# Value and gate blocks 512 columns wide over three token tiles, distance-16 scores copied by ScalarE, and seven raw places in the down-projection

## The chip, the cores and the metric

One core of one Trainium2 chip runs the whole step as one launch. The metric is the device time of that launch in microseconds (us). Time before the change: 1357.84 us, the median of 3 runs (1354.48 to 1359.75).

The engines are named as in the profile: PE is TensorE (matrix products, results in PSUM), PEld its weight loads, DVE is VectorE, ACT is ScalarE, POOL is GpSimd, SP is SyncE, which issues every DMA of this kernel from one in-order queue.

## The reference

One inference step of a one-layer hybrid encoder, on 1024 prompt frames (no history) and 32 sample frames (with states), float32 throughout. `D_MODEL` is 1024, `D_FF` is 2816.

```python
def mixer(xn, ...):                       # xn = rms_norm(x, g)
    proj = xn @ w_in                      # 1024 -> q, k, v, gates of three head groups
    # GLA (6 heads) and HGRN2 (5 heads): gated linear scans in blocks of 64 positions
    scores = jnp.einsum('bihd,bjhd,bijhd->bijh', qc, kc, decay)
    o = (jnp.einsum('bijh,bjhv->bihv', scores, vc)
         + jnp.einsum('bihk,bhkv->bihv', qc * jnp.exp(b), s))
    ...                                   # mLSTM (5 heads): stabilised scan of the same shape
    o = head_rms_norm(o, g) * silu(gate)  # the mLSTM's gate is a sigmoid
    return cat @ w_out, states

def conv_ffn(xn, buf, w_up, conv_w, conv_b, w_down):
    up = xn @ w_up                        # 1024 -> 2 x 2816
    up, buf = causal_dwconv(up, buf, conv_w, conv_b)   # width 3
    gate, val = jnp.split(up, 2, axis=-1)
    return (gelu(gate) * val) @ w_down, buf

x = x + rms_norm(mixer(rms_norm(x)), g_post)
x = x + rms_norm(conv_ffn(rms_norm(x)), g_post)
```

It returns the new frames, the states of the three head groups, and the last rows of both convolutions.

## The kernel before

**Products in three.** Every large product is done with operands split into a high half (a cast to float32r) and a low half (the rest): `mm3` (L88 to L91) issues high x high, high x low and low x high into the same accumulator. `split` (L95 and L98) makes the halves: a cast on ScalarE, a subtraction on VectorE. So each raw weight tile costs one ScalarE and one VectorE instruction before TensorE can use it. In groups 1 and 2 of the input projection the low halves come back from DRAM, where group 0 stored them (`lf_d`, `lt0_d`, `lt_d`; `kept`).

**Input projection, `inproj`.** Tokens are taken in three groups: 0 to 383, 384 to 767, and 768 to 1023 with the 32 sample frames. In each group the normalised frames lie in SBUF as `xh` and `xl`, features on partitions. First comes block 0 of the values for each token tile, then 13 feature blocks (`feat`), then the blocks 1 to 7 of 256 columns: blocks 0 to 3 hold values (`v_d`), 4 to 7 gates (`g_d`). In groups 0 and 1 `vg` goes through the token tiles one by one: 8 slices of the inner dimension, 3 matmuls each, one accumulator (`psb`, tag `big`, three banks in all), with the tile's frames as the stationary operand and 256 weight columns as the moving one. `vg_weights` loads a block as two pieces of [128, 4, 256] floats (`wr` raw, three places; `wh` and `wl`, four places each), and every token tile uses both pieces. `vg_store` reads the accumulator (a ScalarE copy for values; `tanh` into the single buffer `vth` and then a VectorE instruction for gates) and stores 128 x 256 floats. In group 2 `vg_across` does the same blocks with weights as the stationary operand.

**Mixer.** `mixer` handles one tile of 128 tokens, two chunks of 64. The scores within a chunk are built from six distances (32, 16, 8, 4, 2, 1), two to a PSUM tile `sc` of two banks, of which there is one. Per distance, VectorE and ScalarE make decayed copies of q and k, TensorE multiplies them in small tiles, and `copy_scores` puts the result into the matrix `P`: for distance 32 with two ScalarE copies of a rectangle, for the others with a predicated copy under a mask on VectorE (`put`, L808). The mixer of a group runs beside the input projection of the next, that of group 2 beside the output projection.

**Up-projection.** `up_all` runs 22 feature blocks, each as seven products of half size (Strassen's scheme) in 274 and 256 columns, then `up_finish` does the convolution, gelu and product into `h_d`, and sums of quarters of the activations (`s_d`, from tile `st`) and of the down-weights (`t_d`, from tiles `bw`).

**Down-projection, `down_all`.** The first part handles tokens of tiles 0, 8 and 4: 22 blocks, each loading 288 columns of activations (tag `hr`, two places) and a weight row (`wide`, four places, where weight sums are made too). Then `seven` handles the other six token tiles as seven products `p1` to `p7`. Each product has 11 tiles. A raw tile of 896 columns (`r`, tag `y0`, three places) gets 384 columns of activations and 512 of weights in two loads; both are split (`h_halves`, four places in two tags; `weight_halves`, seven places), and three accumulators of 512 columns get three matmuls each. The products run in the order p1, p2, p6, p5, p3, p7, p4; some accumulate onto a bank that an earlier product left, after ScalarE or VectorE has read it.

**Order of instructions.** `merge` and `pump` interleave emission of the mixer with the projections. After that a planner sets the order on every engine: `Graph` takes the dependencies (buffer reuse among them), `play` runs a list schedule with costs from `_cost`, `PRODUCT` (ns of a matmul by columns) and `PACKET` (DMA), the longest remaining path first, and `order` pins the result. In `play`, a load lands at the end of its turn in the DMA queue plus 650 ns.

Of the kernel before, what the change touches and what calls it, by code (L numbers as in the profile page):

```python
# [9 lines left out]
F32 = mybir.dt.float32  # L10
F32R = mybir.dt.float32r
# [20 lines left out]
NCOL = 2 * HW  # L32
# [9 lines left out]
def fcol(u):  # L42
# [24 lines left out]
VG0 = [range(0, 3), range(3, 6), range(6, 8)]  # L67

TC = dict(schedule_with_timeline_sim=True)
IN_NAMES = ["xp", "xs", "w_feat", "w_tok0", "w_tok", "w_out", "w_up", "w_dn", "vecs", "gcols", "grows", "wg",  # L70
            "mconv", "mcache", "fconv", "fcache", "s_gh", "s_c", "s_m", "rowb", "masks", "cf"]
OUTS = [
    ("yp", (SEQ, D)), ("ys", (DEC, D)),
# [6 lines left out]
def body(ctx: ExitStack, tc: tile.TileContext, a: dict):  # L80
    nc = tc.nc
    act, dve, pool, pe, sp = nc.scalar, nc.vector, nc.gpsimd, nc.tensor, nc.sync
# [21 lines left out]
    dr = ctx.enter_context(tc.tile_pool(name="dr", bufs=1, space=DRAM))  # L104
    cp = ctx.enter_context(tc.tile_pool(name="cp", bufs=1))
    psb = ctx.enter_context(tc.tile_pool(name="psb", bufs=3, space=PSUM))
# [6 lines left out]
    pa = pas.enter_context(tc.tile_pool(name="pa", bufs=1, side="right"))  # L113
# [17 lines left out]

    lf_d = dr.tile([13, 128, 8, 128], F32R, name="lf_d")
    lt0_d = dr.tile([128, 8, 282], F32R, name="lt0_d")
    lt_d = dr.tile([7, 2, 128, 4, 256], F32R, name="lt_d")

    def xsrc(t0, n):
        return a["xp"][t0:t0 + n, :] if t0 < SEQ else a["xs"][t0 - SEQ:t0 - SEQ + n, :]
# [25 lines left out]
    vecs = const("vecs_sb", [128, 12], F32, a["vecs"])  # L163
# [180 lines left out]
    def inproj(g, xh, xl, normed, scaled=None):  # L344
# [44 lines left out]

        def vg_weights(blk):  # L390
            parts = [(a["w_tok0"][:, ks[0]:ks[-1] + 1], ks, lt0_d[:, ks[0]:ks[-1] + 1]) for ks in VG0] if not blk else \
                [(a["w_tok"][blk - 1, hf], range(4 * hf, 4 * hf + 4), lt_d[blk - 1, hf]) for hf in range(2)]
            ws = []
            for i, (src, ks, low) in enumerate(parts):
                wh, wl, _ = weights(src, pa, f"wt{g}_{blk}_{i}", [128, len(ks), 256 if blk else 282],
                                    raw=wraw.pop((blk, i), None), eng=dve, low=low, kept=g > 0)
                ws += [(wh[:, k], wl[:, k]) for k in range(len(ks))]
            return ws
# [18 lines left out]
        def vg(blk):  # L417
            ws = vg_weights(blk)
            N = 256 if blk else 282
            for i, (u, off, n) in enumerate(units_of(g)):  # L420
                ps = psb.tile([128, N], F32, tag="big", name=f"pv{u}_{blk}")
                for k in range(8):
                    mm3(ps[:n, :N], (xh[:, k, off:off + n], xl[:, k, off:off + n]), ws[k], k == 0, k == 7)
                if not blk:
                    act.copy(tgs[:n, i, :], ps[:n, 256:])
                vg_store(blk, u, off, n, ps)
                yield

        def vg_across(blks):

# [225 lines left out]
        if sl:  # L656
            yield from vg_across(range(1, 8))
            return
        for blk in range(1, 8):
            yield from vg(blk)  # L660
            if blk == 5 and g < 2:
                for _ in scale_x(g + 1):
                    pass

# [6 lines left out]
    def mixer(u, g, ci0):  # L671
# [176 lines left out]
        def copy_scores(c, sc, lv):  # L848
            s = sc[:, :, 32 * lv:32 * lv + cl // 2]
            if c == levels[0]:  # L850
                for (o, m) in chunks:
                    act.copy(P[o:o + c, :, c:2 * c], s[o:o + c])
            else:
                put(c, s[:n])

# [449 lines left out]
    def down_all(ph, p6, gp):  # L1305
# [40 lines left out]
            return hh, hl  # L1346


        off, w = {}, 0
        for u in FIRST:  # L1350
            off[u] = w
# [2 lines left out]
        banks = [p.tile([128, 512], F32, tag=t, name=f"pd0_{i}", bufs=b) for i, (p, t, b) in enumerate(where)]  # L1354
        pair = []
        for f in range(NF):
            r = ph.tile([128, 288], F32, tag="hr", name=f"hr{f}", bufs=2)
            for u in FIRST:
                n = 128 if u < 8 else DEC
                sp.dma_start(r[:, off[u]:off[u] + n], h_d[f, :, fcol(u):fcol(u) + n])  # L1360
            hh, hl = h_halves(f"0_{f}", w, r, ph, "h")
            wr = praw[0].tile([128, 1024], F32, tag="raw", name=f"wd0_{f}r", bufs=2) if f < 2 else                 wide(f"wd0_{f}r")
            sp.dma_start(wr, a["w_dn"][f])
            wd = [weight_halves(f"wd0_{f}{hf}", wr[:, 512 * hf:512 * hf + 512]) for hf in range(2)]
            pair.append(wr)
            if f % 2:
                if f // 2 >= len(EARLY):
                    sums(f // 2, pair)
                pair = []
            if f == NF - 6:  # L1370
                sp.dma_start(gp, a["grows"][1:2, :].broadcast_to([128, 1024]))
                for u in FIRST:
                    residual(u)
            for d in range(8):
                c = slice(128 * (d % 4), 128 * (d % 4) + 128)
                mm3(banks[d][:, :w], [t[:, c] for t in wd[d // 4]], (hh[:, :w], hl[:, :w]), f == 0, f == NF - 1)
# [27 lines left out]
        def seven(p, ps, first):  # L1404
            ops = []
            for k in range(NP):
                r = ph.tile([128, NCOL], F32, tag="y0", name=f"r{p}_{k}", bufs=3)
                sp.dma_start(r[:, :384], ASRC[p](k))
                sp.dma_start(r[:, 384:896], BSRC[p](k))
                hh, hl = h_halves(f"{p}_{k}", 384, r[:, :384], *((ph, "h") if k % 2 else (p6, "g")))  # L1410
                wd = weight_halves(f"wd{p}_{k}", r[:, 384:896])
                ops.append((k, hh, hl, wd))
                if k == NP - 2:
                    continue
                for i in range(3):
                    c = slice(128 * i, 128 * i + 128)
                    for (j, hh, hl, wd) in ops:
                        mm3(ps[i], (hh[:, c], hl[:, c]), wd, first and j == 0, j == NP - 1, skip_group_check=True)
                ops = []
                if k % 3 == 0 and todo:  # L1420
                    todo.pop(0)()
# [54 lines left out]
    def merge(main, nmain, nside):  # L1476

        done = 0
        for i, _ in enumerate(main):
            want = (i + 1) * nside // nmain  # L1480
            pump(want - done)
            done = want
# [3 lines left out]
        return chain_of(*[mixer(u, g, c) for (u, c) in us[-1:] + us[:-1]]) if us[-1][0] == 8 else \  # L1486
            chain_of(*[mixer(u, g, c) for (u, c) in us])

    NMIX, NIN = 14, 12 + 2 + 24

    for g in range(3):
        xs_ = norm_tiles(g)
        n_side = (0, 3 * NMIX - 6, 3 * NMIX)[g]
        pump(1000)
        scaled = scale_x(0) if g == 0 else None
        if scaled:
            next(scaled)
            next(scaled)
        merge(inproj(g, *xs_, norm_group(g, *xs_), scaled), NIN, n_side)
        if g == 0:  # L1500
            mixer_zeros()
        side.append(mixers(g))
# [92 lines left out]
AHEAD = {"mx": 10000., "psm": 10000., "pdx0": 1400., "pdx1": 700., "pdw0": 1400., "pdw1": 700., "pt": 130000.}  # L1595
ENGINES = ("PE", "DVE", "Activation", "Pool", "SP")
WINDOW = 3413.3
PRODUCT = {512: 232., 384: 175.5, 288: 133.5, 282: 131.5, 274: 126.5, 256: 118.}
PACKET = ((4, 9), (32, 9), (128, 13), (256, 18), (512, 27), (1024, 46), (1536, 65), (2048, 84), (4096, 159), (8192, 330), (1 << 16, 2640))
TABLES = {"Ln": 5, "Gelu_apprx_tanh": 11, "Exp": 0, "Tanh": 0, "Square": 0}  # L1600

# [267 lines left out]
def play(g, tail, change, slack=None):  # L1869
# [32 lines left out]
    while True:  # L1902
# [30 lines left out]
        if e == "SP":  # L1933
            free[e] = t + own
            queue = max(t + 1400, queue) + d
            stop = queue + 650
        elif e == "PE":
            d, wide, m, cl, (row, sums) = mm[n]
            if mode not in (None, m):
                t = max(t, max(cells) + (93 if mode == (128, 128) else 45))  # L1940
            mode, t = m, max([t] + [cells[c] for c in cl])
            if wide:
                free[e] = clock.run(t, d)
                cells = [free[e]] * 16
                stop = free[e] + 166
            else:
                f = clock.factor(t)
                for c in cl:
                    cells[c] = t + d * f
                clock.add(t, 14)  # L1950
                free[e] = t + 14 * f
                stop = t + d * f + 168
        else:
            if e == "DVE" and lock:
                t = max(t, port["Pool"])
                port["DVE"] = t + d
            if e == "Pool" and lock == 1:
                port["Pool"] = t + d
            if g.table[n] not in (None, table):
                table = g.table[n]  # L1960
                t += 1283
            free[e], stop = t + own, t + d
# [26 lines left out]
def _layout(i):  # L1989
# [12 lines left out]
    wt = np.hstack([wv, np.hstack([gr, hg, mo])[:, of_plane]]).reshape(2, 4, 128, 8, 256)  # L2002
    wt = wt.transpose(3, 0, 2, 1, 4)
    w_tok = np.ascontiguousarray(wt[1:])
    w_tok0 = np.hstack([wv[:, :256], gg, mf, mi]).reshape(8, 128, 282).transpose(1, 0, 2)
    w_out = np.asarray(i["w_out"])[0][of_plane].reshape(8, 128, 1024)
    w_up = np.ascontiguousarray(np.asarray(i["ffn_w_up"])[0].reshape(8, 128, 44, 128).transpose(2, 1, 0, 3))
# [58 lines left out]
    for pl, (t, r0, dk) in enumerate(PLANES):  # L2066
        cf[r0:r0 + dk, 832 + 11 * t + pl] = 1.0
        if t < 2:
            cf[r0:r0 + dk, 876 + 2 * t + (r0 // 32 % 2 if dk == 32 else 0)] = 1.0
    r = dict(xp=np.asarray(i["x_prompt"])[0], xs=np.asarray(i["x_sample"])[0], w_feat=w_feat, w_tok0=w_tok0, w_tok=w_tok, w_out=w_out,  # L2070
             w_up=w_up, w_dn=w_dn, vecs=vecs, gcols=gcols, grows=grows, wg=wg, mconv=mconv, mcache=mcache, fconv=fconv,
             fcache=fcache, s_gh=s_gh, s_c=s_c, s_m=s_m, rowb=rowb, masks=masks, cf=cf)
    return {k: np.ascontiguousarray(v) for k, v in r.items()}
# [44 lines left out]
```

## Time and profile before

| | us |
|---|---|
| median of 3 runs | 1357.84 |
| the profiled execution | 1356.24 |
| its span, first to last instruction | 1354.4 |
| TensorE busy (modelled ends) | 1303.9 |
| VectorE busy | 1039.2 |
| ScalarE busy | 710.6 |

The stages in the profiled span: group 0 of the input projection up to some 160 us, group 1 to 340, group 2 to 475, output projection to 645, up-projection to some 1090, first part of the down-projection to 1171, the seven products to 1347, and the last sums and stores.

How to read the lines: in a table by stage, each engine has its busy us and, in brackets, its instructions; then the granted TensorE clock (1.00 is full), the mean busy share of the 16 DMA engines, and GB/s. A line of a tile has count, then shortest, median and longest duration in ns, the first and the last start in us, and the shapes. A line of waits reads: who waited, for whom, us in total, times, longest. In the chain, each piece has its start, its length, and what ran; "issue" is time in which the engine waited for nothing that the profile shows. In a timeline, x3 merges three neighbours. `pv` is the accumulator of a value or gate block, `pdx`, `pdy` and `pdw` are those of the seven products, `rp` the raw tile there, `wdp` and `hlp` or `hhp` its halves, `hr` the raw activations of the first part.

### The profile page before, as it was taken

Reading aid. Unit: us, or ns where it says so; the run is one execution under the profiler, and the core shown is the slowest. Engines: PE = TensorE matmul, PEld = TensorE weight load, DVE = VectorE, ACT = ScalarE, POOL = GpSimd, SP = SyncE. Lnnn points to the kernel's source line nnn. Section 1 sums busy time; section 2 is a strip of 40 time slices with the busy share of each in tenths; the row PEclk is TensorE's granted clock in tenths of the full one; section 3 lists DMA queues with packets and bytes.
Section 4 is the critical chain, followed back from the end, with each engine's and each line's share of the span. In section 5 each row is a group of like instructions: output and inputs, shape, how many; then the busy total and the mean of one; then the engine's idle time right before and its main releaser. Section 6 shows DMA issues by size and latency. Waiting matters only on the chain.

```text
span 1354.4 us, 30370 instructions
## 1 busy us (share of the span) xinstructions
PE 1303.9 (96%) x11977; PEld 1207.9 (89%) x11977; DVE 1039.2 (77%) x1884; ACT 710.6 (52%) x1400; POOL 181.9 (13%) x331
## 2 busy tenths in 40 slices
PE   6999999999999999999899999999999999998997
PEld 5999999998898887678899999999999999886775
DVE  6795549757889468878899988888888877755576
ACT  5654556545576554436754544545545454555554
POOL 2010100100102112222012211111111110000011
PEclk9999999999999999999999999999999999999998
DMA  9899869976898964635156623323223189786675
GB/s 327 260 330 332 266 243 333 301 260 203 287 305 288 331 231 121 202 95 171 69 199 230 215 97 109 102 87 119 80 87 119 71 275 290 261 265 192 218 248 205
DMA packets 148422, 285.24 MB, mean 211 GB/s; under 512 B 30039, under 2 KB 84471, under 8 KB 148279
## 3 DMA queue, kind: packets, MB, share of 16 engines
q1 hardware_dynamic: 148279, 283.30, 62.2%
q8 instruction: 94, 1.54, 0.5%
q14 instruction: 49, 0.40, 0.1%
HBM read 201.90 MB, written 81.34 MB: 209 GB/s over the span
## 4 chain that ended last, share of the span: by engine, by line
PE 69%; DMA 14%; DVE 9%; ACT 4%; issue 3%; SPq 1%; POOL 0%; DVEq 0%; ACTq 0%; POOLq 0%
PE pux L91 4%; PE pux L89 4%; PE pux L90 4%; PE pv L89 4%; PE pv L91 4%; PE pv L90 4%; DMA rp<-t_d 4%; PE pf L89 3%; PE pf L91 3%; PE pf L90 3%; PE puw L90 3%; PE puw L91 3%; PE puw L89 3%; DMA rp<-in_w_dn 2%; PE zp L89 2%
## 5 line engine op out<-in xcount | busy, mean ns | idle before, releaser
L1250 DVE SCALAR_TENSOR_TENSOR y<-uu,fconv_sb,y 128x1060 f32<-128x1060 f32 x88 | 115.8, 1320 | 7.9 <-ACT y L1248 7.4
L98 DVE TENSOR_TENSOR wdp<-rp,wdp 128x512 fp32r<-128x512 f32 x77 | 53.2, 691 | 56.2 <-ACT wdp L95 55.9
L95 ACT CAST wdp<-rp 128x512 fp32r<-128x512 f32 x77 | 47.7, 620 | 70.4 <-DMA rp<-t_d 39.0
L1248 ACT ACTIVATE y<-uu,fconv_sb 128x1060 f32<-128x1060 f32 x44 | 56.1, 1278 | 25.9 <-POOL uu L1245 21.5
L1196 ACT COPY c<-pux 128x274 f32<-128x274 f32 (+1 forms) x132 | 46.3, 381 | 33.9 <-PE pux L91 30.1
L926 POOL TENSOR_TENSOR hrs<-hss,mhalf 128x5 f32<-128x5 f32 (+3 forms) x27 | 35.8, 1330 | 175.3 <-DVE hss L925 172.6
L89 PE MATMUL pv<-wt_0h,xh 128*128 128x256 f32 (+2 forms) x195 | 53.8, 297 | 2.6 <-DVE xl L309 1.3
L91 PE MATMUL pv<-wt_0h,xl 128*128 128x256 f32 (+2 forms) x195 | 51.7, 288 | 0.0
L90 PE MATMUL pv<-wt_0l,xh 128*128 128x256 f32 (+2 forms) x195 | 51.5, 287 | 0.0
L89 PE MATMUL pdx<-wdp,hhp 128*128 128x512 f32 x132 | 44.8, 404 | 6.7 <-ACT hhp L95 4.6
L89 PE MATMUL pv<-wt_1h,xh 128*128 128x256 f32 (+2 forms) x195 | 49.1, 288 | 0.0
L91 PE MATMUL pv<-wt_1h,xl 128*128 128x256 f32 (+2 forms) x195 | 48.6, 288 | 0.0
L1245 POOL COPY uu<-fcache_sb 128x2 f32<-128x2 f32 x44 | 23.4, 531 | 186.1 <-DVE uu L1201 186.1
L90 PE MATMUL pv<-wt_1l,xh 128*128 128x256 f32 (+2 forms) x195 | 48.3, 288 | 0.0
L98 DVE TENSOR_TENSOR hlp<-rp,hhp 128x384 fp32r<-128x384 f32 x77 | 41.8, 552 | 5.4 <-ACT hhp L95 2.9
L90 PE MATMUL pdx<-wdp,hhp 128*128 128x512 f32 x132 | 43.9, 395 | 0.0
L91 PE MATMUL pdx<-wdp,hlp 128*128 128x512 f32 x132 | 42.9, 395 | 0.1
L95 ACT CAST hhp<-rp 128x384 fp32r<-128x384 f32 x77 | 38.4, 511 | 5.8 <-PE pdx L90 3.1
L89 PEld LDWEIGHTS pv<-wt_0h,xh 128*128 128x128 f32 (+1 forms) x195 | 35.2, 189 | 4.6 <-DVE xl L309 1.6
L211 POOL TENSOR_SCALAR gss<-gss 128x1 f32<-128x1 f32 (+1 forms) x9 | 7.4, 817 | 233.7 <-ACT gjk L1324 158.2
L89 PEld LDWEIGHTS pdx<-wdp,hhp 128*128 128x128 f32 x132 | 24.8, 191 | 13.9 <-ACT hhp L95 6.7
L808 DVE COPY_PREDICATED P<-masks_sb,sc 128x352 f32<-128x352 int32 (+1 forms) x44 | 29.8, 678 | 8.8 <-PE sc L773 8.3
(1781 smaller groups left out, 5144.4 us busy)
## 6 DMA issues: line engine op xcount, KB each, us to landing
h_d<-y SPq DMA_DIRECT2D x22, 530.0 KB, 5.1
rp<-t_d SPq DMA_DIRECT2D x44, 256.0 KB, 3.8
wt_0r<-in_w_tok SPq DMA_DIRECT2D x21, 512.0 KB, 5.9
wt_1r<-in_w_tok SPq DMA_DIRECT2D x21, 512.0 KB, 5.0
rp<-in_w_dn SPq DMA_DIRECT2D x33, 256.0 KB, 3.7
rp<-s_d SPq DMA_DIRECT2D x44, 192.0 KB, 3.9
wt_0l<-lt_d SPq DMA_DIRECT2D x14, 512.0 KB, 4.7
wt_1l<-lt_d SPq DMA_DIRECT2D x14, 512.0 KB, 5.8
```

The source lines that it names most:

```text
L89: pe.matmul(ps, lh[0], rh[0], start=first, stop=False, **kw)
L90: pe.matmul(ps, lh[0], rh[1], start=False, stop=False, **kw)
L91: return pe.matmul(ps, lh[1], rh[0], start=False, stop=last, **kw)
L95: act.copy(hi, src)
L98: (eng or pool).tensor_tensor(lo, src, hi.bitcast(F32), op=ALU.subtract)
L211: pool.tensor_scalar(out, ss, other, EPS, op0=ALU.add, op1=ALU.add)
L808: dve.copy_predicated(dst, mk_.broadcast_to([n, 11, *mk_.shape[2:]]), src)
L926: pool.tensor_tensor(rs[:n, h0:h0 + nh], ss[:n, h0:h0 + nh], mhalf[:n, :nh], op=ALU.pow)
L1196: act.copy(t, ps)
L1245: pool.tensor_copy(u[:, GAP_S:GAP_S + 2], fcache[:, j, :])
L1248: act.activation(y, u, AF.Identity, scale=fconv[:, j, 2:3], bias=fconv[:, j, 3:4])
L1250: dve.scalar_tensor_tensor(y, uu[i][:, s:s + NCOL], fconv[:, j, s:s + 1], y, op0=ALU.mult, op1=ALU.add)
```

## The change

- In groups 0 and 1 the blocks 2 to 7 are done in pairs (`vg_pair`): 512 columns at once, the three token tiles together in three accumulators. The weights come in four pieces of [128, 2, 512] per pair from a second copy of the weights in that layout (`w_tokw`), and their low halves are kept in `lw_d`. Group 2 reads its low halves from slices of `lw_d`. `merge` counts more and smaller steps.
- For full token tiles, the scores at distance 16 are copied into `P` by four ScalarE copies of 16 rows each.
- The raw tiles of the seven products rotate through seven places: three of tag `y0`, two of `bw`, one of `y1`, one of `st`. The raw activations of the first part take four places: two of `hr` and two of `bw`.
- The planner's numbers for a matmul change by a few ns, and a load lands 1250 ns after its turn in the queue rather than 650.

```diff
-    lt_d = dr.tile([7, 2, 128, 4, 256], F32R, name="lt_d")
+    lt_d = dr.tile([2, 128, 4, 256], F32R, name="lt_d")
+    lw_d = dr.tile([3, 2, 128, 4, 512], F32R, name="lw_d")
...
-                [(a["w_tok"][blk - 1, hf], range(4 * hf, 4 * hf + 4), lt_d[blk - 1, hf]) for hf in range(2)]
+                [(a["w_tok"][blk - 1, hf], range(4 * hf, 4 * hf + 4), lt_d[hf] if blk == 1 else
+                  lw_d[blk // 2 - 1, hf, :, :, 256 * (blk % 2):256 * (blk % 2) + 256])
+                 for hf in range(2)]
...
+        def vg_pair(blk):
+            us = units_of(g)
+            pss = [psb.tile([128, 512], F32, tag="big", name=f"pv{u}_{blk}") for (u, off, n) in us]
+            for q in range(4):
+                wh, wl, _ = weights(a["w_tokw"][blk // 2 - 1, q], pa, f"ww{g}_{blk}_{q}", [128, 2, 512], eng=dve,
+                                    low=lw_d[blk // 2 - 1, q // 2, :, 2 * (q % 2):2 * (q % 2) + 2], kept=g > 0)
+                for (u, off, n), ps in zip(us, pss):
+                    for j in range(2):
+                        k = 2 * q + j
+                        mm3(ps, (xh[:, k, off:off + n], xl[:, k, off:off + n]), (wh[:, j], wl[:, j]), k == 0, k == 7)
+                    if q < 3:
+                        yield
+                        continue
+                    for e in range(2):
+                        vg_store(blk + e, u, off, n, ps[:, 256 * e:256 * e + 256])
+                    yield
...
-        for blk in range(1, 8):
-            yield from vg(blk)
-            if blk == 5 and g < 2:
+        yield from vg(1)
+        for blk in (2, 4, 6):
+            yield from vg_pair(blk)
+            if blk == 4 and g < 2:
...
+            elif c == 16:
+                for o in range(0, n, 32):
+                    b = o % 64
+                    act.copy(P[o:o + c, :, b + c:b + 2 * c], s[o:o + c, :, b // 2:b // 2 + c])
             else:
                 put(c, s[:n])
...
+        places = [("y0", 3), ("bw", 2), ("y0", 3), ("y1", 1), ("y0", 3), ("bw", 2), ("st", 1)]
+        count = [0]
+
+        def raw(name):
+            t, b = places[count[0] % 7]
+            count[0] += 1
+            return ph.tile([128, 896], F32, tag=t, name=name, bufs=b)
...
-            r = ph.tile([128, 288], F32, tag="hr", name=f"hr{f}", bufs=2)
+            r = ph.tile([128, 288], F32, tag="hr", name=f"hr{f}", bufs=2) if f % 4 < 2 else \
+                ph.tile([128, 288], F32, tag="bw", name=f"hr{f}", bufs=2)
...
-                r = ph.tile([128, NCOL], F32, tag="y0", name=f"r{p}_{k}", bufs=3)
+                r = raw(f"r{p}_{k}")
...
-        merge(inproj(g, *xs_, norm_group(g, *xs_), scaled), NIN, n_side)
+        merge(inproj(g, *xs_, norm_group(g, *xs_), scaled), (12 + 2 + 6 + 36, 12 + 2 + 24)[g == 2], n_side)
...
-PRODUCT = {512: 232., 384: 175.5, 288: 133.5, 282: 131.5, 274: 126.5, 256: 118.}
+PRODUCT = {512: 227.5, 384: 175., 288: 132.5, 282: 131., 274: 127., 256: 119.5}
...
-            stop = queue + 650
+            stop = queue + 1250
```

More of the change, by code (lines that the diff above doesn't have):

```diff
@@ L69 @@
 TC = dict(schedule_with_timeline_sim=True)
-IN_NAMES = ["xp", "xs", "w_feat", "w_tok0", "w_tok", "w_out", "w_up", "w_dn", "vecs", "gcols", "grows", "wg",
+IN_NAMES = ["xp", "xs", "w_feat", "w_tok0", "w_tok", "w_tokw", "w_out", "w_up", "w_dn", "vecs", "gcols", "grows", "wg",
             "mconv", "mcache", "fconv", "fcache", "s_gh", "s_c", "s_m", "rowb", "masks", "cf"]
@@ L1487, in mixers @@
             chain_of(*[mixer(u, g, c) for (u, c) in us])
-    NMIX, NIN = 14, 12 + 2 + 24
+    NMIX = 14
     for g in range(3):
@@ L2004, in _layout @@
     w_tok = np.ascontiguousarray(wt[1:])
+    w_tokw = np.ascontiguousarray(w_tok[1:].reshape(3, 2, 2, 128, 2, 2, 256).transpose(0, 2, 4, 3, 5, 1, 6)).reshape(3, 4, 128, 2, 512)
     w_tok0 = np.hstack([wv[:, :256], gg, mf, mi]).reshape(8, 128, 282).transpose(1, 0, 2)
@@ L2069, in _layout @@
             cf[r0:r0 + dk, 876 + 2 * t + (r0 // 32 % 2 if dk == 32 else 0)] = 1.0
-    r = dict(xp=np.asarray(i["x_prompt"])[0], xs=np.asarray(i["x_sample"])[0], w_feat=w_feat, w_tok0=w_tok0, w_tok=w_tok, w_out=w_out,
+    r = dict(xp=np.asarray(i["x_prompt"])[0], xs=np.asarray(i["x_sample"])[0], w_feat=w_feat, w_tok0=w_tok0, w_tok=w_tok, w_tokw=w_tokw, w_out=w_out,
              w_up=w_up, w_dn=w_dn, vecs=vecs, gcols=gcols, grows=grows, wg=wg, mconv=mconv, mcache=mcache, fconv=fconv,
```

## The prediction

> **What bounds the kernel now.** I read the page first (busy shares, chain), then the busy time of each engine by stage, then the chain and the waits of the last stage alone.
>
> ```profile
> span 1354.4 us, 30370 instructions
> ...
> PE 1303.9 (96%) x11977; PEld 1207.9 (89%) x11977; DVE 1039.2 (77%) x1884; ACT 710.6 (52%) x1400; POOL 181.9 (13%) x331
> ...
> PE 69%; DMA 14%; DVE 9%; ACT 4%; issue 3%; SPq 1%; POOL 0%; DVEq 0%; ACTq 0%; POOLq 0%
> ```
>
> ```profile
> core 0: us, PE busy (x) PEld busy (x) DVE busy (x) ACT busy (x) POOL busy (x), PEclk, DMA share, GB/s
> 100.00:160.00 60.00, 59.47 (x565) 58.41 (x564) 31.75 (x64) 27.51 (x61) 0.42 (x1) 1.00 0.95 321
> 200.00:250.00 50.00, 49.25 (x621) 46.93 (x619) 46.72 (x102) 32.23 (x63) 6.75 (x10) 1.00 0.94 312
> 400.00:450.00 50.00, 46.66 (x733) 43.72 (x732) 41.41 (x106) 29.87 (x74) 10.66 (x11) 0.99 0.86 281
> 480.00:540.00 60.00, 58.71 (x647) 47.58 (x646) 49.45 (x108) 29.40 (x67) 11.33 (x16) 1.00 0.58 190
> 660.00:1090.00 430.00, 429.66 (x3498) 429.41 (x3497) 380.82 (x571) 213.11 (x378) 74.63 (x168) 1.00 0.36 127
> 1090.00:1171.00 81.00, 78.74 (x594) 77.36 (x593) 62.49 (x106) 41.36 (x78) 3.76 (x8) 1.00 0.90 298
> 1171.00:1347.00 176.00, 166.25 (x726) 133.19 (x724) 111.89 (x192) 93.73 (x194) 11.36 (x15) 0.99 0.69 224
> ```
>
> TensorE is the bound nearly everywhere, so there are two ways to gain: fewer nanoseconds of matmul, or fewer holes between them. The value and gate blocks at 100 to 160 us have no holes (59.47 of 60). The up-projection (660 to 1090) has none and isn't touched. The last stage, the seven products of the down-projection (1171 to 1347), has the most, 9.75 us, with the DMA engines at only 0.69. The chain of that stage alone (1170 to the end), with one turn of its loop, says why:
>
> ```profile
> by line: DMA rp<-t_d 25.9%; DMA rp<-in_w_dn 17.0%; DVE hlp L98 8.1%; issue 7.3%; PE pdx L89 6.3%; PE pdx L90 5.8%; PE pdx L91 5.7%; ACT wdp L95 4.8%; DMA rp<-h_d 2.4%; DMA rp<-s_d 1.9%; DVE fr L1335 1.6%; DVE wdp L98 1.6%; ACT hhp L95 1.2%;
> ...
> 1178.34 0.44 PE ptxw L1389 x4
> ...
> 1239.22 4.26 DMA rp<-t_d
> ...
> 1245.76 4.26 DMA rp<-t_d
> ...
> 1265.74 3.60 DMA rp<-in_w_dn
> 1269.36 0.63 ACT wdp L95
> 1270.07 0.55 issue
> 1270.62 0.56 DVE hlp L98
> 1271.20 2.81 DMA rp<-in_w_dn
> ```
>
> The reader sees a buffer loop: a raw tile lands, ScalarE casts it, VectorE takes the rest, the place comes free, and only then is the load three tiles on issued. A turn takes 5.46 us (1265.74 to 1271.20) or 6.54 (1239.22 to 1245.76), for three tiles.
>
> **Seven raw places: the term that carries the sum.** What a tile costs TensorE comes from matmul starts, 512 columns first, then 256:
>
> ```profile
> 1256.50 0.39 PE L89 MATMUL pdw<-wdp,hhp 128*128 128x512 f32 x1
> ...
> 1267.38 0.84 PE L89 MATMUL pdw<-wdp,hhp 128*128 128x512 f32 x3
> ```
>
> ```profile
> 142.82 0.40 PE L89 MATMUL pv<-wt_0h,xh 128*128 128x256 f32 x2
> ...
> 148.16 0.40 PE L89 MATMUL pv<-wt_1h,xh 128*128 128x256 f32 x2
> ```
>
> 48 matmuls lie between the first two rows: 10.88 / 48 = 0.227 us. 45 lie between the others: 5.34 / 45 = 0.1187 us. A tile feeds nine 512-wide matmuls, 2.04 us, three tiles 6.13. The loop's turn lies on both sides of that, and with three places a short turn can't be saved up for a long one. What is lost:
>
> ```profile
> L89 PE MATMUL pdx<-wdp,hhp x132: 387/389/628, 1171.7 to 1345.9; 128*128 128x512 f32 x132
> ...
> L91 PE MATMUL pdx<-wdp,hlp x132: 387/389/628, 1172.4 to 1346.3; 128*128 128x512 f32 x132
> ...
> L1439 ACT COPY cu<-pdx x3: 578/583/592, 1247.7 to 1252.8; 128x512 f32<-128x512 f32 x3
> ```
>
> From 1171.7 to 1346.5 are 174.8 us. Seven products of 11 tiles of 9 matmuls are 693 x 0.227 = 157.3. The 24 transposes in the stretch take 0.11 each (0.44 for four), 2.6, and the last matmuls of the part before some 0.7 (an estimate, five narrower ones). So 14.2 us are holes. With seven places the loop may take 14.3 us, over twice the longest turn shown; behind the raw tiles the code has seven places for split weights and four for split activations, so the casts can run ahead too. What remains is the hand-over of accumulators between products, six of them; I charge each one copy (0.58 us): 3.5. Gain 14.2 - 3.5 = **10.7 us**; bounds 0 and 14.2. Part of it is clock:
>
> ```profile
> 1320.00:1330.00 10.00, 7.88 (x28) 6.31 (x28) 8.24 (x14) 5.97 (x15) 0.00 (x0) 0.83 1.00 362
> ```
>
> After the longest hole the granted clock fell to 0.83 over 10 us; without the hole that doesn't come. Bandwidth suffices: a tile is 448 KB in 2.04 us, 225 GB/s, and this row shows 362 at a share of 1.00. The number of loads and their bytes is unchanged, so SyncE's queue issues no more than before.
>
> The new places must be free in time, and the first part has a wait of its own:
>
> ```profile
> L1265 SPq DMA_DIRECT2D s_d<-st x11: 319/320/430, 703.0 to 1127.0; - x11
> ```
>
> ```profile
> ACT hh L95 <- DMA hr<-h_d: 9.0, 8, 2.7
> ```
>
> `st` is last stored at 1127, 45 us before the stage needs it. The activations of the first part (`hr`) get four places for two, which could take some of its 2.26 us of idle TensorE. Against that, up to four more raw tiles (1.8 MB, 5.6 us at 325 GB/s, which is 224 / 0.69) are now loaded into a stretch whose DMA share is 0.90. Bounds -2.3 and +5.6; I take 0, since the planner puts the loads of the earlier part first.
>
> **Blocks 512 wide.** Groups 0 and 1 had 6 blocks x 3 tiles x 24 matmuls each, 864 of 256 columns. Now 432 of 512. Two narrow ones cost 0.2373, a wide one 0.227: 432 x 0.0106 = **4.6 us** less. [...] Weight pieces stay 12 per group of the same size, loads, low-half stores and result stores too; each piece is now used for 18 x 0.227 = 4.1 us and dropped, where two had to stay for a whole block.
>
> What it adds: the three accumulators of the pool are all held by a pair and end within 2.7 us of each other.
>
> ```profile
> L101 ACT ACTIVATE vth<-pv x24: 363/384/396, 122.3 to 320.4; 128x256 f32<-128x256 f32 x24
> L412 DVE SCALAR_TENSOR_TENSOR vg<-vth,pv x18: 353/418/422, 123.6 to 306.5; 128x256 f32<-128x256 f32 x12, 128x192 f32<-128x192 f32 x6
> ```
>
> ```profile
> L324 ACT CAST wt_1h<-wt_1r 128x1024 fp32r<-128x1024 f32 x14 | 14.7, 1050 | 4.4 <-PE pv L91 3.8 <-PE pv L90 0.6
> ```
>
> A gate tile costs 2 x (0.384 + 0.418) = 1.6 us in series (`vth` has one buffer), three tiles 4.8. The next pair wants the third bank 24 x 0.227 = 5.4 us after the first tile ends. That just fits, until a 1.05 us weight cast stands before it in ScalarE's queue. I charge a third of a cast at each of six pair ends: **+2.0 us**; bounds 0 and 6 x 4.8.
>
> **Scores at distance 16.** Per full token tile one predicated copy leaves VectorE and four ScalarE copies come, eight times.
>
> ```profile
> L808 DVE COPY_PREDICATED P<-masks_sb,sc x44: 329/542/967, 165.9 to 584.3; 128x352 f32<-128x352 int32 x40, 32x176 f32<-32x176 int32 x4
> L852 ACT COPY P<-sc x17: 295/444/448, 164.8 to 571.7; 32x352 f32<-32x352 f32 x16, 16x176 f32<-16x176 f32 x1
> ```
>
> VectorE gives up 8 x 0.54 = 4.3 us, ScalarE takes 32 x 0.295 = 9.4 (the one copy of that shape). VectorE is the fuller engine in these stages (46.72 of 50 at 200 to 250, ScalarE 32.23), yet the score bank now waits for ScalarE, with the exponentials of the next level queued behind. Bounds -4.3 and +9.4; I take **-1.0**, a quarter of VectorE's relief.
>
> **Edits at nothing.** Group 2 reads its low halves in runs of 1 KB for 4 KB: 6.3 MB; hidden by a DMA share of 0.86, and at half the rate it would be 22 us of DMA time, of which some 19 fit into the 135 us of that group (340 to 475): 0 to +3. The planner counts a load's landing 0.6 us later and matmuls a few ns otherwise; this reorders all queues. Its price lies within the idle TensorE time of the mixer stretches shown, 0.75 + 3.34 + 1.29: -4 to +4; I take 0.
>
> **Sum.** -10.7 - 4.6 + 2.0 - 1.0 = -14.3. The profiled execution took 1356.24 us (span 1354.4 and 1.84 around it), 1.6 under the median: 1341.9 as profiled, **1343.5** as a median.
>
> **Rivals.** *More than that:* the reordering also fills the mixer's holes and the first part's, and hand-overs are free: 3.5 + 2.3 + 4 more, 1334. For it: the planner's landing was too early. Chance 0.17.
>
> *The seven places only move the wait:* the first part is pushed by the whole 5.6 us and accumulators hold up the rest, so the last stage gives back all 10.7: 1354. For it: DMA share 0.90 just ahead. Against: 0.69 where the holes are. Chance 0.14.
>
> *ScalarE becomes the mixer's chain:* the copies cost 9.4 instead of -1.0: 1354. Against: ScalarE is busy 49 to 64% there. Chance 0.05.
>
> *Slower, by the pair ends:* TensorE stops at each until its banks are read.
>
> ```profile
> DVE vg L412 <- ACT vth L101: 18.8, 9, 4.7
> ```
>
> Without their charge the sum is -16.3, so six ends pass +6.8 us from 3.85 us each; at the 4.7 of the longest wait of this kind they cost 28.2 and the kernel takes 1370. Against: in group 1 the mixer's matmuls can fill. [...] Chance 0.07.
>
> **Numbers.** The forecast has 0.57 and its own range 1337 to 1351. About 0.5%, 6.8 us, is what a measurement of this kernel can tell from no change. Faster (under 1351.0): 0.57 + 0.17 = 0.74; within: 0.14 + 0.05 = 0.19; slower (over 1364.6): 0.07. The range 1331 to 1356 takes in the larger gain and the two cases at 1354.
>
> **What would show it.** Right: the last stage some 164 us long for 174.8, its chain led by TensorE rather than by `rp` loads, clock 1.00 throughout; 432 wide `pv` matmuls 0.227 us apart; ScalarE copies to `P` x49. Wrong: TensorE idle before `pv` until ScalarE's `vth` or VectorE's `vg`; the part from 1090 to 1171 longer; TensorE before the scores waiting for L852's successor.

## The result and the profile after

The changed kernel took 1347.03 us (median of 6 runs, 1343.83 to 1349.7), the kernel before 1356.16 (6 runs, 1352.63 to 1360.38) on the same chip: ratio 0.9935, 95% interval 0.991 to 0.9961. The profiled execution took 1343.83 (span 1342.0), 3.2 under its median. Single runs of one kernel differ by 6 to 17 us. So stages are read from profiles, each of one execution, and what an edit is worth from the ratios; these are turned into us with the median of some 1354.8 that the kernel before had beside the experiments (0.001 is 1.35 us, and the intervals are 2 to 3 us either way).

The page of the changed kernel, then its busy time by stage:

```profile
span 1342.0 us, 29591 instructions
...
PE 1297.5 (97%) x11545; PEld 1185.1 (88%) x11545; DVE 1034.6 (77%) x1876; ACT 723.3 (54%) x1432; POOL 179.3 (13%) x331
...
PE 80%; DVE 8%; DMA 7%; ACT 3%; issue 2%; SPq 1%; POOL 0%; DVEq 0%; ACTq 0%; POOLq 0%
```

```profile
core 0: us, PE busy (x) PEld busy (x) DVE busy (x) ACT busy (x) POOL busy (x), PEclk, DMA share, GB/s
100.00:160.00 60.00, 58.18 (x298) 48.11 (x297) 28.17 (x51) 27.43 (x54) 0.00 (x0) 1.00 0.92 307
200.00:250.00 50.00, 49.88 (x724) 47.58 (x722) 45.87 (x105) 33.10 (x63) 5.73 (x9) 1.00 0.92 305
480.00:540.00 60.00, 57.11 (x611) 45.27 (x606) 47.04 (x102) 29.28 (x69) 10.39 (x14) 1.00 0.55 183
1090.00:1171.00 81.00, 78.66 (x594) 77.26 (x593) 60.75 (x103) 40.25 (x78) 3.72 (x8) 1.00 0.91 302
1171.00:1335.00 164.00, 163.73 (x747) 135.85 (x745) 116.26 (x198) 97.25 (x198) 11.79 (x16) 1.00 0.72 237
```

The last row is what the change was forecast to do: the seven products have no holes left (163.73 of 164; before, 166.25 of 176), and the chain's share of DMA went from 14% to 7%. The first and third rows are what was not: the stretch of group 0's wide blocks now has 1.8 us of idle TensorE where there was 0.5 (it lies just behind them, at 151.5 and 157.1), and that of the output projection 2.9 where there was 1.3. The chain of the last stage, and the first and last matmul of the products:

```profile
by line: PE pdx L90 16.9%; PE pdx L89 16.9%; PE pdx L91 16.8%; PE pdw L90 8.7%; PE pdw L91 8.7%; PE pdw L89 8.7%; PE pdy L89 4.3%; PE pdy L90 4.3%; PE pdy L91 4.3%; DVE fr L1360 2.0%; PE pd L91 1.0%; PE pd L90 0.9%; PE ptxw L1423 0.8%; PE p
```

```profile
L89 PE MATMUL pdx<-wdp,hhp x132: 387/389/477, 1172.9 to 1333.9; 128*128 128x512 f32 x132
...
L91 PE MATMUL pdx<-wdp,hlp x132: 387/389/477, 1173.3 to 1334.3; 128*128 128x512 f32 x132
```

No load stands in that chain any more: TensorE runs from one matmul to the next. 1172.9 to 1334.3 are 161.4 us, where 1171.7 to 1346.3 were 174.6. So the last stage gave 13.2 us, more than the 12.4 between the two profiled executions; everything ahead of it together lost 1.2.

### The profile page after: what moved, and what is told of

The parts are those of the page before. It is cut to its first block, busy times and chain, and to the rows that moved or that the text cites. A ratio compares the mean times of both kernels' runs of the same rounds, so it can differ in the third digit from the quotient of the medians.

```text
span 1342.0 us, 29591 instructions
## 1 busy us (share of the span) xinstructions
PE 1297.5 (97%) x11545; PEld 1185.1 (88%) x11545; DVE 1034.6 (77%) x1876; ACT 723.3 (54%) x1432; POOL 179.3 (13%) x331
## 4 chain that ended last, share of the span: by engine, by line
PE 80%; DVE 8%; DMA 7%; ACT 3%; issue 2%; SPq 1%; POOL 0%; DVEq 0%; ACTq 0%; POOLq 0%
PE pux L89 5%; PE pux L90 5%; PE pux L91 5%; PE pv L89 4%; PE pv L91 4%; PE pv L90 4%; PE pf L89 3%; PE pf L90 3%; PE pf L91 3%; PE puw L91 3%; PE puw L89 3%; PE puw L90 3%; PE pdx L90 2%; PE pdx L89 2%; PE pdx L91 2%; PE sc L794 2%
## 5 line engine op out<-in xcount | busy, mean ns | idle before, releaser
L98 DVE TENSOR_TENSOR hlp<-rp,hhp 128x384 fp32r<-128x384 f32 x77 | 42.6, 556 | 37.2 <-ACT hhp L95 11.8
L90 PE MATMUL pdx<-wdp,hhp 128*128 128x512 f32 x132 | 43.2, 390 | 0.0
L89 PE MATMUL pdx<-wdp,hhp 128*128 128x512 f32 x132 | 42.8, 391 | 0.0
L829 DVE COPY_PREDICATED P<-masks_sb,sc 128x352 f32<-128x352 int32 (+1 forms) x36 | 25.4, 705 | 10.9 <-PE sc L794 10.7
L90 PE MATMUL pd<-hl,wd 128*128 128x288 f32 x176 | 31.0, 297 | 1.6 <-DVE hl L98 1.5
L1226 DVE TENSOR_TENSOR uu<-c,puw 128x274 f32<-128x274 f32 (+1 forms) x44 | 19.0, 431 | 17.3 <-PE puw L91 16.3
L89 PE MATMUL pd<-hh,wd 128*128 128x288 f32 x176 | 31.2, 296 | 0.7 <-ACT hh L95 0.7
L1269 POOL COPY uu<-uu 128x2 f32<-128x2 f32 x44 | 10.9, 248 | 145.9 <-DVE uu L1226 145.7
L91 PE MATMUL pd<-hh,wd 128*128 128x288 f32 x176 | 30.4, 294 | 0.0
L1278 DVE TENSOR_TENSOR y<-y,y 128x1060 f32<-128x1060 f32 x22 | 27.8, 1261 | 3.1 <-ACT y L1277 1.2
L377 DVE SCALAR_TENSOR_TENSOR y<-pc,mconv_sb,y 128x384 f32<-128x384 f32 (+1 forms) x45 | 26.1, 581 | 4.7 <-ACT dcs L601 2.3
L794 PEld LDWEIGHTS sc<-Qz,Ld 64*64 64x64 f32 (+1 forms) x1344 | 24.9, 133 | 5.5 <-issue 2.9
```

What stands on the lines that cost most here:

```text
L89: pe.matmul(ps, lh[0], rh[0], start=first, stop=False, **kw)
L90: pe.matmul(ps, lh[0], rh[1], start=False, stop=False, **kw)
L91: return pe.matmul(ps, lh[1], rh[0], start=False, stop=last, **kw)
L98: (eng or pool).tensor_tensor(lo, src, hi.bitcast(F32), op=ALU.subtract)
L377: dve.scalar_tensor_tensor(y, pc[:, s:s + L], mconv[:, j, s:s + 1], y, op0=ALU.mult, op1=ALU.add)
L794: return lambda: pe.matmul(ps, lh, rh, start=start, stop=stop, skip_group_check=True)
```

## The experiments

All were timed in five rounds against the kernel before; the last column is the time from the first to the last `pdx` matmul of the profiled execution. The ratio is not that of the medians: for the raw places alone the medians differ by 11.8 us, and the ratio says 8.9.

| kernel | median us | ratio to before (95%) | `pdx`, us |
|---|---|---|---|
| the full change | 1347.0 | 0.9935 (0.991 to 0.9961) | 161.4 |
| raw places alone (seven and `hr`) | 1343.0 | 0.9934 (0.991 to 0.9957) | 163.0 |
| pairs alone | 1363.9 | 1.007 (1.0044 to 1.0097) | 176.1 |
| scores alone | 1349.3 | 0.9964 (0.9945 to 0.9983) | 173.2 |
| planner's numbers alone | 1347.6 | 0.9955 (0.9939 to 0.9972) | 166.3 |
| full, without pairs | 1336.1 | 0.9854 (0.9831 to 0.9877) | 162.3 |
| full, without the raw places | 1348.2 | 0.995 (0.9931 to 0.9968) | 165.0 |
| full, without the scores | 1347.9 | 0.9935 (0.9913 to 0.9957) | 161.8 |
| full, without the planner's numbers | 1351.4 | 0.9975 (0.9953 to 0.9997) | 164.5 |
| full, pairs in group 0 only | 1345.8 | 0.9932 (0.9908 to 0.9956) | 161.6 |
| full, pairs in group 1 only | 1338.0 | 0.9875 (0.9851 to 0.9899) | 161.5 |
| four raw places alone | 1358.5 | 1.0019 (0.9996 to 1.0041) | 175.2 |
| planner's matmul costs alone | 1359.0 | 1.002 (0.9996 to 1.0045) | 172.2 |

**One part at a time, on the kernel before.** The raw places:

```diff
-                r = ph.tile([128, NCOL], F32, tag="y0", name=f"r{p}_{k}", bufs=3)
+                r = raw(f"r{p}_{k}")        # seven places; and hr in four
```

> The kernel before with only the raw places changed: seven for the seven products, four for the first part's activations. Theory (buffer loop): the time from the first pdx matmul to the last falls from 174.8 to 161 to 162 us, as in the full change, and the whole time falls by 11 to 13 us, so this part alone is worth more than the full change. Rival (the loads are bound by DMA bandwidth, and the rest of the change made room for them): the seven products stay above 168 us and the gain is under 7 us.

They alone made the last stage 163.0 us and the kernel 0.66% faster (8.9 us): the buffer loop, though not more than the full change gives. The pairs alone (`vg_pair` in groups 0 and 1, `lw_d`, the step count in `merge`):

> The kernel before with only the 512-wide pairs in groups 0 and 1 (planner's numbers as before). Theory (the matmul time is saved, and what eats it in the full change is a hole from the order of the queues, not the pairs): 432 wide matmuls at 0.227 us, the blocks save 4.6 us of matmul time, and the whole time falls by 2 to 4 us. Rival (pairs cost as much as they save, by the three accumulators they hold): TensorE idles before pv or at the group's end for 4 us or more, and the time is within 1 us of before or above it.

Slower by 0.7%, 9.5 us, as the rival said: the one part that costs. The ScalarE copies at distance 16 alone:

> The kernel before with only the distance-16 scores copied by ScalarE. Theory (VectorE is relieved of 4.3 us, a quarter of which shows): 0 to -2 us. Rival (ScalarE's 9.4 us lie on the mixer's chain): +3 us or more, with the stretch from 160 to 635 us longer.

Faster by 0.36% (4.9 us), more than either theory had. The planner's numbers alone (`PRODUCT` and 650 to 1250):

> The kernel before with only the planner's numbers changed (matmul costs, landing of loads 600 ns later); the instructions are the same, in another order. Theory (order is worth little by itself): within 2 us of before. Rival (the order of the queues is worth as much as any part of the change): 4 us or more either way, with holes of 1 us and more at other places than before.

Faster by 0.45% (6.1 us), as the rival said, and the place of the gain is the last stage, with its three places as before (its chain from 1170 on):

```profile
by line: DMA rp<-t_d 17.0%; PE pdw L89 8.2%; PE pdw L91 8.1%; PE pdw L90 8.0%; PE pdx L91 6.8%; PE pdx L90 6.8%; PE pdx L89 6.5%; PE pdy L89 4.0%; PE pdy L90 4.0%; PE pdy L91 4.0%; issue 3.2%; DVE hlp L98 3.0%; DMA rp<-h_d 2.8%; ACT wdp L95
```

Loads from `t_d` still hold 17% of that chain (25.9% before), those from `in_w_dn` are out of it (17.0% before). So the same holes can be closed by room and, in part, by order.

**One part taken out of the full change.** The edits are those above, backwards.

> The full change without the 512-wide pairs (blocks 256 wide as before). Theory (the pairs alone cost 9 us, and cost as much inside the full change): 1335 to 1339 us, 9 us faster than the full change, ratio to before near 0.987. Rival (what the pairs cost alone was the accident of one order of the queues, and in the full order they save their matmul time): 1347 to 1351, no faster than the full change.

> The full change without the new raw places (three raw tiles, two places for the first part's activations). Theory (the planner's later landing by itself took 8 us out of the seven products, so the two parts overlap): the first pdx to the last takes 165 to 168 us, 4 to 6 us more than in the full change, and the time is 1351 to 1354. Rival (the places carry it alone): 173 to 176 us for the products and 1358 to 1361 in all.

> The full change without the ScalarE copies of the distance-16 scores (VectorE's predicated copy as before). Theory (the copies are worth 5 us by themselves and as much here): 1351 to 1353 us. Rival (they are worth 1 us, and the 5 us measured alone were the order): 1346 to 1349.

> The full change with the planner's old numbers. Theory (with seven places the seven products are bound by TensorE whatever the order, so the planner's numbers are worth little there; what they are worth must lie in the stages before 1090 us): 161 to 163 us from the first pdx to the last, whole time within 3 us of the full change. Rival (they are worth 6 to 7 us here too, as alone): 1353 us or more, with the loss between 160 and 640 us.

Without the pairs the kernel takes 1336.1, 0.9854 of before: it beats both kernels. Taking out the raw places costs 2.0 us, not 8.9, since the new order already shortens the stage to 165.0; that 2.0, and the nothing that taking out the scores costs, can't be told from zero. Taking out the planner's numbers costs 5.4, more than the 3 that were expected, and 164.5 us of `pdx` say that part of it lies in the last stage. The single parts sum to -8.9 + 9.5 - 4.9 - 6.1 = -10.4, and the whole is -8.8; but that they nearly agree proves little, since the places and the planner's numbers close the same holes and are worth less together.

**Which pairs cost.** The full change with pairs in one group only (`merge` counts steps to match; both keep the low halves in `lw_d`):

```diff
-        yield from vg(1)
-        for blk in (2, 4, 6):
-            yield from vg_pair(blk)
-            if blk == 4 and g < 2:
+        yield from vg(1)
+        for blk in range(2, 8):
+            if g == 0:                       # the other kernel: g == 1
+                if blk % 2 == 0:
+                    yield from vg_pair(blk)
+            else:
+                yield from vg(blk)
+            if blk == 5 and g < 2:
```

> The full change, but group 1 takes its blocks 2 to 7 singly, 256 columns wide, as before; only group 0 has pairs. The full change took 1347.0 and without any pairs 1336.1. Theory M (the loss lies in group 1: wide products next to the mixer's small ones gain nothing and make the mixer late, so that the output projection starts late): about 1335, some 1.8 less than without pairs from 216 wide matmuls at 232 ns for 432 at 120.5, plus about 1 for the pair ends; the output projection and the first pux start as early as without pairs (479 and 627, within 2). Theory H (the loss lies in group 0: the 2.8 us hole at 88.5 and the lower clock behind it, and a later start of the mixer): 1345 to 1347, with the hole at 88 and the first pux at 636. If both share it: 1339 to 1343.

> The full change, but group 0 takes its blocks 2 to 7 singly; only group 1 has pairs. Theory M: 1345 to 1348, first pux about 636 as in the full change. Theory H: 1336 to 1338, first pux at 628. If both share it: 1339 to 1343, and the two losses, of this kernel and of the one with pairs in group 0 alone, add up to the 10.9 us of the full change.

Theory H holds: pairs in group 0 alone cost 0.9932 - 0.9854, 10.6 us; in group 1 alone 2.8, which can't be told from zero. Theory M, by which wide products among the mixer's small ones are the loss, falls. The stretch ahead of group 0's wide blocks shows a first difference. Busy time from 85 to 95 us: the full change, pairs alone, no pairs, pairs in group 0, pairs in group 1, one row each.

```profile
85.00:95.00 10.00, 7.33 (x47) 7.10 (x46) 7.68 (x13) 5.01 (x10) 3.42 (x4) 0.84 1.01 342
```

```profile
85.00:95.00 10.00, 7.32 (x53) 7.10 (x52) 7.67 (x14) 5.06 (x10) 3.37 (x4) 0.92 0.99 330
```

```profile
85.00:95.00 10.00, 9.96 (x82) 9.76 (x81) 7.87 (x14) 5.76 (x11) 0.92 (x4) 1.00 1.03 350
```

```profile
85.00:95.00 10.00, 7.36 (x52) 7.13 (x51) 7.65 (x14) 4.58 (x10) 3.42 (x4) 0.89 1.03 344
```

```profile
85.00:95.00 10.00, 10.00 (x83) 9.82 (x82) 7.88 (x14) 5.53 (x11) 0.96 (x5) 1.00 1.02 352
```

The three with pairs in group 0 have 2.7 us of idle TensorE there, and a lower clock; the two without have neither. The same hole of 2.6 to 2.7 us stands in all six kernels with pairs in group 0, and in none of the other eight. The timeline of the full change at that place (start, length, engine, line, operation):

```profile
84.65 1.05 ACT L95 CAST ww_0h<-ww_0r 128x1024 fp32r<-128x1024 f32 x1 [0.38 <-PE pf L90]
...
85.71 1.05 ACT L95 CAST ww_1h<-ww_1r 128x1024 fp32r<-128x1024 f32 x1
...
87.66 1.22 DVE L98 TENSOR_TENSOR ww_0l<-ww_0r,ww_0h 128x1024 fp32r<-128x1024 f32 x1
...
88.80 1.22 DVE L98 TENSOR_TENSOR ww_1l<-ww_1r,ww_1h 128x1024 fp32r<-128x1024 f32 x1
...
89.93 0.55 DVE L382 SCALAR_TENSOR_TENSOR mo<-th,y 128x384 f32<-128x384 f32 x1
...
90.52 0.55 DVE L584 TENSOR_TENSOR e<-r_bb,r_m 5x384 f32<-5x384 f32 x1
...
91.11 0.21 ACT L586 ACTIVATE r_dc<-e 5x6 f32<-5x6 f32 x1 [2.00 <-DVE e L584]
...
91.37 0.80 PE L599 MATMUL mi<-r_dc,cf_sb 5*128 5x6 f32 x5 [2.67 <-ACT r_dc L586]
```

The pair's weight pieces are split on VectorE at 87.66 and 88.80. `mo` and `e`, small steps of the mixer's gates, queue behind them; ScalarE's `r_dc` waits for `e`, and the tiny product `mi` at L599, which stands in TensorE's order ahead of the next `pv`, waits for `r_dc`: 2.67 us. In the full change without pairs VectorE splits pieces of the same size at about the same time, but `e` stands ahead of them:

```profile
85.88 0.56 DVE L564 TENSOR_TENSOR e<-r_bb,r_m 5x384 f32<-5x384 f32 x1
...
86.54 1.22 DVE L98 TENSOR_TENSOR wt_0l<-wt_0r,wt_0h 128x1024 fp32r<-128x1024 f32 x1
```

So the largest wait that the pairs bring is not at a pair's end, where the prediction looked, but ahead of the first pair, and by these lines it is one of order: the pair's weights are split before a small step on which TensorE's next instructions hang. A kernel with pairs and `e` moved ahead wasn't run. The clock just before the hole and just behind it:

```profile
85.00:88.50 3.50, 3.50 (x29) 3.48 (x27) 3.50 (x5) 2.28 (x3) 0.60 (x1) 1.00 1.04 374
```

```profile
91.30:95.00 3.70, 3.63 (x18) 3.61 (x19) 1.44 (x4) 2.16 (x6) 0.79 (x3) 0.58 0.97 359
```

At 0.58 for 3.7 us, TensorE lost another 1.6 us (an estimate, 3.7 x 0.42): a narrow `pv` matmul took 0.214 us to the next start there (92.69 to 94.83), and 0.119 ahead of the hole (85.80 to 88.41). The kernel with pairs in group 0 alone loses as much by that estimate: over 85 to 97 us its granted clock is 0.86, 1.7 us of 12. Hole and clock so cost 4.3 us at this place. They don't explain the 10.6, though. From 85 to 167 us TensorE idles 5.6 us with pairs in group 0 and 4.3 without any, since the waits at the change of groups are 2.6 us with them and 3.4 without; and the wide blocks save some 2 us. The first matmul of each stage tells where the loss shows:

| first start, us | no pairs | group 0 | group 1 | full |
|---|---|---|---|---|
| group 2's features (`pf`) | 338.5 | 338.7 | 336.6 | 341.9 |
| output projection (`zp`) | 479.4 | 481.6 | 476.5 | 484.1 |
| up-projection (`pux`) | 627.2 | 637.9 | 630.1 | 636.6 |

With pairs in group 0, only 0.2 us are lost at the start of group 2, and 8.5 us of the 10.7 come between 480 and 638, long after the pairs. That stretch with pairs in group 0, then without any:

```profile
481.60:637.90 156.30, 147.95 (x1498) 115.80 (x1497) 116.90 (x222) 73.03 (x165) 36.46 (x39) 0.97 0.49 160
```

```profile
479.40:627.20 147.80, 143.22 (x1513) 112.15 (x1512) 117.40 (x223) 74.38 (x167) 32.66 (x39) 1.00 0.52 168
```

TensorE idles 8.4 us for 4.6, and the granted clock of 0.97 is, by the same estimate, 4.7 us of 156.3: together the 8.5. The waits of the longest hole name a late tile of the mixer (TensorE's wait first, then VectorE's before it):

```profile
PE og L798 <- DVE P L833: 3.0, 1, 3.0
```

```profile
DVE cat L953 <- DMA gt<-g_d: 5.7, 1, 5.7
```

A gate tile's load lands late, VectorE stands 5.7 us before it with the score copies behind, and TensorE waits 3.0. But the kernel with the planner's numbers alone, which has no pairs, shows the same two waits, of 5.4 and 2.4 us, so they can't be the pairs' alone. Yet the loss goes with the pairs: from the first `zp` to the first `pux` takes 152.5 to 157.6 us in all seven kernels that have pairs in either group, and 146.4 to 150.2 in the seven that have none. By which path it comes isn't shown. All seven with pairs also read group 2's low halves from `lw_d` in runs of 1 KB, and no kernel has one without the other. So some 8 us of group 0's loss stay open. In the full change half of the 9.4 us lost at the first `pux` (4.7) come in this stretch.

**How many places.** Four raw places, nothing else:

```diff
+        places = [("y0", 3), ("y0", 3), ("y0", 3), ("y1", 1)]
```

> The kernel before with four raw places in the seven products instead of three (a fourth of tag y1); nothing else. Theory L (the load, cast, split and free loop of 5.5 to 6.5 us is the only limit, and four tiles are 8.2 us of TensorE): nearly all of the gain of seven places, 1343 to 1345, first to last pdx 163 to 165 against 174.6. Rival (long turns come in a row, when SyncE's queue is full of other loads, and want depth to be ridden out): half of it, 1348 to 1350, first to last pdx 168 to 170.

Both theories fall: no gain at all (1.0019, 0.9996 to 1.0041), and 175.2 us from the first to the last `pdx`. The chain of that stage changed, yet the two long holes did not go. Its chain, and two of its stretches:

```profile
by line: DMA rp<-t_d 11.2%; PE pdx L89 9.7%; PE pdx L91 9.5%; PE pdx L90 9.4%; DMA rp<-in_w_dn 7.8%; issue 4.4%; ACT wdp L95 3.7%; DVE hlp L98 3.7%; DVE wdp L98 1.4%; DVE fr L1335 1.2%; SPq L1416 1.0%; ACT gjk L1324 0.8%; SPq L1417 0.8%; DV
```

```profile
1220.00:1230.00 10.00, 6.27 (x24) 4.77 (x24) 6.41 (x12) 4.46 (x10) 0.00 (x0) 0.92 0.58 191
1230.00:1240.00 10.00, 10.00 (x41) 8.14 (x40) 6.46 (x12) 5.27 (x10) 0.00 (x0) 0.91 0.55 179
...
1320.00:1330.00 10.00, 7.17 (x25) 5.58 (x24) 8.84 (x16) 7.12 (x16) 0.00 (x0) 0.83 1.05 400
```

From 1240 to 1290 the holes went (49.56 us busy of 50, before 47.09). But the waits at 1220 and 1320 got longer (6.27 and 7.17 busy; before 7.53 and 7.88), and each brings the lower clock. Counting a turn of the loop against the tiles it may cover (5.5 to 6.5 us against 8.2 for four) fits the steady part and misses these two waits; that loads come late there one after the other, and that seven places bridge this, is how I read it and isn't shown. Where between four and seven it turns wasn't run, nor seven without the two places more for `hr`.

**Which of the planner's numbers.** The matmul costs alone:

```diff
-PRODUCT = {512: 232., 384: 175.5, 288: 133.5, 282: 131.5, 274: 126.5, 256: 118.}
+PRODUCT = {512: 227.5, 384: 175., 288: 132.5, 282: 131., 274: 127., 256: 119.5}
```

> The kernel before with the planner's new matmul costs alone; a load lands 650 ns after its turn as before. Both numbers together took 1347.6 for 1354.6. Theory T (the landing carries it: loads are issued earlier in SyncE's order and casts stand where their data has come): no change, 1353 to 1357, first to last pdx 173 to 175. Rival (the matmul costs carry it): 1347 to 1349, first to last pdx 166 to 168. A new order alone, of whatever sort, moves the time by some us: 1350 to 1353 would say that.

Nothing gained (1.002, 0.9996 to 1.0045), as theory T said, though 1359.0 and 172.2 us from the first to the last `pdx` lie a little outside its figures. So the landing 0.6 us later carries the planner's gain, alone or with the costs; the landing by itself wasn't run.

## Why the prediction was right, and where it was not

The forecast was 1343.5; 1347.0 came. The sign, the place of the gain and its mechanism were right. Between the two profiled executions 12.4 us went, where 14.3 were forecast; by the ratio it is 8.8. That the sum came so near is in good part luck: the pairs cost 12 to 14 us more than forecast, and the planner's numbers, forecast at nothing, made up for about half of that (5 to 6 us).

*Seven raw places, -10.7.* Right in mechanism; the last stage gave 13.2 us, but with the planner's numbers in it: the places alone made it 11.6 us shorter (163.0). What I charged for the hand-over of accumulators, 3.5, isn't there: in the full change no wait of a `pdx`, `pdy` or `pdw` matmul is left. The clock is 1.00 throughout. What the forecast didn't have is the overlap with the planner's numbers, which get 8.3 us out of the same stage with three places.

*First part, 0.* Right: 1090 to 1171 has 78.66 us of busy TensorE for 78.74. So the rival in which the seven places only move the wait there is out.

*Blocks 512 wide, -4.6: the step of the sum that failed.* I took the spacing of the seven products, 0.227 us, for that of the wide `pv`. The full change, first and last of 24 matmuls in a row in group 0:

```profile
104.07 0.39 PE L89 MATMUL pv<-ww_0h,xh 128*128 128x512 f32 x1
...
109.41 0.39 PE L89 MATMUL pv<-ww_3h,xh 128*128 128x512 f32 x1
```

5.34 / 23 = 0.232. Against two narrow ones, 0.2374, that saves 5 ns and not 10.6: 2.3 us over all 432. In group 1 hardly any of this is left. At the changes between small tiles and full ones a wide one takes longer:

```profile
253.34 0.40 PE L90 MATMUL pv<-ww_0l,xh 128*128 128x512 f32 x1
253.66 1.16 PE L794 MATMUL sc<-Qz,Ld 64*64 64x64 f32 x64
254.65 0.52 PE L794 MATMUL sm<-mqk 64*64 64x64 f32 x10
255.10 0.50 PE L91 MATMUL pv<-ww_1h,xl 128*128 128x512 f32 x1
255.44 0.39 PE L91 MATMUL pv<-ww_0h,xl 128*128 128x512 f32 x1
255.67 0.62 PE L89 MATMUL pv<-ww_1h,xh 128*128 128x512 f32 x2
```

The last wide one before the scores takes 0.32 us to the next start, the first one behind them 0.34, the one after that 0.23. So 0.1 us goes at each side of this change; why isn't shown. In the kernel before, the narrow ones pay as much at such changes (0.21 us from 248.99 to the scores, 0.22 from 245.69 behind them, for 0.12), so this doesn't tell why group 1 gains less. TensorE's busy time in `pv` alone, in both groups, first in the full change, then without pairs:

```profile
85.00:150.00 65.00, 60.69 (x288) 50.57 (x288) 3.22 (x8) 6.84 (x19) 0.97 0.92 312
238.00:321.00 83.00, 65.45 (x288) 47.80 (x288) 3.26 (x8) 6.99 (x19) 1.00 0.82 272
```

```profile
85.00:150.00 65.00, 61.78 (x504) 60.44 (x504) 3.56 (x9) 7.50 (x20) 1.00 0.98 332
238.00:321.00 83.00, 65.59 (x502) 61.35 (x501) 3.62 (x9) 7.50 (x20) 1.00 0.87 288
```

That is 1.1 us saved in group 0 and 0.1 in group 1. The first row also has the 72 narrow matmuls of the block ahead of the pairs, some of them at the low clock behind the hole (0.97 on the whole). From 98.1 to 149.8, at full clock, 216 wide and 13 narrow ones take 51.7 us, where the 432 narrow ones without pairs take 52.5; 13 narrow ones are 1.5, so the wide ones save about 2 us in group 0 and some 2 of the 4.6 in all. My row had the right width and came from another stage: 0.227 us there, 0.232 here. A spacing must be taken from the same stage, not only from the same width.

*Six pair ends, +2.0.* Right in size (six thirds of 1.05 us are 2.1):

```profile
PE pv L89 <- ACT vg L407: 1.4, 3, 0.6
...
PE pv L89 <- ACT vth L101: 1.2, 1, 1.2
```

Of these 2.6 us, 1.2 (at 152.7) and 0.6 (at 278.2) stand at the end of a pair, 1.8 in all; the rest lies in the narrow block at 157.7 and in group 2. The missing terms are the wait ahead of the first pair, 2.7 us of hole and an estimated 1.6 of clock, and the longer output projection, which stays open. The whole edit was forecast at -2.6 and is +9.5 alone, +11.0 in the full change. The rival "slower by the pair ends" had the sign of this edit right, and its place wrong.

*Scores, -1.0.* 49 ScalarE copies to `P`, as forecast:

```profile
L877 ACT COPY P<-sc x32: 290/297/300, 205.2 to 575.0; 16x176 f32<-16x176 f32 x32
L873 ACT COPY P<-sc x17: 278/444/450, 202.8 to 572.6; 32x352 f32<-32x352 f32 x16, 16x176 f32<-16x176 f32 x1
```

Alone they gave -4.9 us, VectorE's whole relief of 4.3 and some; in the full change 0. TensorE waits for none of them in the full change, so "ScalarE becomes the mixer's chain" is out.

*Planner's numbers, 0.* Wrong: -6.1 alone, 5.4 lost when taken out. I looked for their price in the mixer's holes; they act mainly in the seven products (8.3 us there when alone), where the order of loads decides. The rival "more than that" had their sign and the free hand-overs right.

*Low halves in runs of 1 KB, 0.* Group 2, from its first `pf` to the first `zp`, took 142.2 us for 144.1; but 146.8 in the kernel with the pairs alone, and 140.9 in the full change without them. A loss of 1 to 3 us, as the bounds had it, isn't excluded.

## What to carry to other kernels

A part of a change that is forecast to gain by a better instruction shape must be charged for what its operands displace: here the pair's weight pieces got ahead of two small steps in VectorE's queue, and a saving of 2 us in group 0 came with a 2.7 us hole and an estimated 1.6 us of clock, and with a longer stage far behind it, by a path that wasn't found. Buffer depth and issue order close the same holes, so their gains don't add, and a turn-time count says too little about depth: by it four places should have done, and they gave nothing where seven gave 8.9 us. Take a bundle of edits apart even where it is faster: this one hid an edit that cost 11 us, and without it the kernel takes 0.9854 of the time before.

## What the runs showed of the hardware that I had not expected

A wide matmul takes 0.227 us to the next start in the seven products and 0.232 in the value and gate blocks, with the same shape and clock. Behind a hole of 2.67 us the granted clock was 0.58 over the next 3.7 us; the lower clock at the wait at 1220 in the kernel with four places cost as much (0.92, then 0.91 over 10 us each: an estimate of 1.7 us). In the kernel with pairs in group 0 alone the clock was 0.51 behind a single hole of 1.70 us:

```profile
570.60:574.00 3.40, 1.70 (x30) 1.25 (x28) 3.08 (x9) 3.27 (x10) 1.29 (x2) 1.00 1.06 317
574.00:577.50 3.50, 3.50 (x32) 2.66 (x34) 2.18 (x8) 1.49 (x4) 0.00 (x0) 0.51 1.02 401
```

The clock was still 1.00 ahead of the first hole (85 to 88.5 us) and over the stretch that holds the second (570.6 to 574).
